# A row normalization with a loop of tiles: statistics combined by bn_aggr on VectorE instead of on GpSimd, in groups of four rows, and the last store issued as two DMAs

## The chip, the cores and the metric

The kernel runs on one core of a Trainium2 chip. The metric is the device time of the program in microseconds; the time before is the median of three runs. DVE is VectorE, ACT is ScalarE, POOL is GpSimd, SP is SyncE. TensorE does nothing here. 16 DMA engines move data between the memory that holds `x` and `out` and the on-chip memory of 128 partitions.

## The reference

```python
batch, seq, dim = 32, 512, 1024          # x: float32, eps = 1e-5
mean = np.mean(x, axis=-1, keepdims=True)
var = np.var(x, axis=-1, keepdims=True)
return ((x - mean) / np.sqrt(var + eps)).astype(np.float32)
```

There are 32 x 512 = 16384 rows of 1024 numbers, each normalized by itself: 67.11 MB are read and 67.11 MB are written.

## The kernel before

The rows are cut into 18 tiles (`TILES`): fifteen of 8 rows per partition, then one of 4 and two of 2. A tile of K rows has K x 128 rows of `x`, and each partition holds K rows that lie side by side in memory, so a load or a store is one DMA with one run of K x 4 KB per partition. Loads go into a ring of 32 rows per partition (`XRING`, four tiles of 8), results into a ring of their own of 16 rows (`YRING`, two tiles of 8). A load is issued by SP (line 124), a store by ACT's queue (line 129). The order of the instructions on each engine is the order of the program; nothing is rescheduled.

The loop in line 123 goes over the tiles. For each it issues the load, calls `group` for up to `GROUP` = 8 rows at a time (so once per tile), and issues the store. `group` does this:

- Line 77: DVE runs `bn_stats` twice per row, on 512 numbers each. Each call leaves six numbers: for the even and for the odd half of its input a count, a mean and a sum of squared deviations. A row so has four means and four sums.
- Lines 88 to 103: POOL combines them with nine instructions for all rows of the group. `pool_sum` adds four terms in two steps; the negated mean, the deviations of the four means from it, their squares times 256 and the sums of squares follow.
- Line 105: ACT takes the square root of the variance plus eps. Line 109: DVE takes the reciprocal. Line 111: POOL multiplies negated mean and reciprocal.
- Line 113: ACT writes each row as row x `rstd` + `nmr`, one instruction of 1024 numbers per partition and row.

A load waits until ACT and DVE have read the rows that it overwrites, four tiles back. The first `yr` of a tile waits until the store two tiles back has landed. On DVE the reciprocal of a tile stands ahead of the statistics of the next one, so DVE is at most one group ahead of ACT.

Of the kernel before, what the change touches and what calls it, by code (L numbers as in the profile page):

```python
# [1 line left out]

# [4 lines left out]


TILES = (8, 8, 8, 8, 8, 8, 8, 8, 8, 8, 8, 8, 8, 8, 8, 4, 2, 2)  # L10

XRING = 32
YRING = 16

GROUP = 8


def place(tiles, ring):

    plan, row, pos = [], 0, 0  # L20
    for K in tiles:
        if pos + K > ring:
            pos = 0
        plan.append((K, row, pos))
        row += K
        pos += K
    return plan


@with_exitstack  # L30
def kernel(
    ctx: ExitStack,
    tc: tile.TileContext,
    x: bass.AP,
    eps: bass.AP,
    out: bass.AP,
):
    nc = tc.nc
    P = nc.NUM_PARTITIONS
    eps_val = float(eps) if not isinstance(eps, bass.AP) else 1e-5  # L40

    x2 = x.flatten_outer_dims()
    o2 = out.flatten_outer_dims()
    N, D = x2.shape
    BN_MAX = nc.vector.BN_STATS_FMAX
    NSUB = D // BN_MAX
    assert sum(TILES) * P == N

    rings = ctx.enter_context(tc.tile_pool(name="rings", bufs=1))
    st = ctx.enter_context(tc.tile_pool(name="st", bufs=4))  # L50

    fdt = mybir.dt.float32
    AF = mybir.ActivationFunctionType
    ALU = mybir.AluOpType

    xr = rings.tile([P, XRING, D], fdt)
    yr = rings.tile([P, YRING, D], fdt)
    eps_t = rings.tile([P, 1], fdt)

    def rows_of(a, row, K):  # L60
        return a[row * P : (row + K) * P].rearrange("(p k) d -> p k d", p=P)

    def pool_sum(o, terms):
        G = terms.shape[1]
        half = st.tile([P, GROUP, 2], fdt, name="half")
        nc.gpsimd.tensor_tensor(  # L66
            out=half[:, :G], in0=terms[:, :, 0:2], in1=terms[:, :, 2:4], op=ALU.add
        )
        nc.gpsimd.tensor_tensor(  # L69
            out=o, in0=half[:, :G, 0], in1=half[:, :G, 1], op=ALU.add  # L70
        )

    def group(xs, ys, G):
        stats = st.tile([P, GROUP, NSUB, 6], fdt, name="stats")
        for k in range(G):
            for s in range(NSUB):
                nc.vector.bn_stats(  # L77
                    out=stats[:, k, s, :],
                    in_=xs[:, k, s * BN_MAX : (s + 1) * BN_MAX],
                )  # L80

        H = 2 * NSUB
        parts = stats[:, :G].rearrange("p g s (h c) -> p g (s h) c", h=2)
        mean4, m2 = parts[:, :, :, 1], parts[:, :, :, 2]
        nmean = st.tile([P, GROUP], fdt, name="nmean")
        dev = st.tile([P, GROUP, H], fdt, name="dev")
        ss = st.tile([P, GROUP], fdt, name="ss")
        pool_sum(nmean[:, :G], mean4)
        nc.gpsimd.tensor_scalar(  # L89
            out=nmean[:, :G], in0=nmean[:, :G], scalar1=-1.0 / H, scalar2=None, op0=ALU.mult  # L90
        )
        nc.gpsimd.tensor_tensor(  # L92
            out=dev[:, :G],
            in0=mean4,
            in1=nmean[:, :G].unsqueeze(2).to_broadcast([P, G, H]),
            op=ALU.add,
        )
        nc.gpsimd.tensor_mul(out=dev[:, :G], in0=dev[:, :G], in1=dev[:, :G])  # L98
        nc.gpsimd.tensor_scalar(  # L99
            out=dev[:, :G], in0=dev[:, :G], scalar1=float(D // H), scalar2=None, op0=ALU.mult  # L100
        )
        nc.gpsimd.tensor_tensor(out=dev[:, :G], in0=dev[:, :G], in1=m2, op=ALU.add)  # L102
        pool_sum(ss[:, :G], dev[:, :G])
        std = st.tile([P, GROUP], fdt, name="std")
        nc.scalar.activation(  # L105
            out=std[:, :G], in_=ss[:, :G], func=AF.Sqrt, bias=eps_t, scale=1.0 / D
        )
        rstd = st.tile([P, GROUP], fdt, name="rstd")
        nc.vector.reciprocal(out=rstd[:, :G], in_=std[:, :G])  # L109
        nmr = st.tile([P, GROUP], fdt, name="nmr")  # L110
        nc.gpsimd.tensor_mul(out=nmr[:, :G], in0=nmean[:, :G], in1=rstd[:, :G])  # L111
        for k in range(G):
            nc.scalar.activation(  # L113
                out=ys[:, k, :],
                in_=xs[:, k, :],
                func=AF.Identity,
                bias=nmr[:, k : k + 1],
                scale=rstd[:, k : k + 1],
            )

    with tc.manual_schedule():
        nc.vector.memset(eps_t, eps_val)  # L122
        for (K, row, xp), (_, _, yp) in zip(place(TILES, XRING), place(TILES, YRING)):
            nc.sync.dma_start(out=xr[:, xp : xp + K, :], in_=rows_of(x2, row, K))
            for g in range(0, K, GROUP):
                G = min(GROUP, K - g)
                a, b = xp + g, yp + g
                group(xr[:, a : a + G, :], yr[:, b : b + G, :], G)
            nc.scalar.dma_start(out=rows_of(o2, row, K), in_=yr[:, yp : yp + K, :])  # L129


# [1 line left out]
_INS = ['x', 'eps']  # L133
_OUTS = [((32, 512, 1024), 'float32')]

_NUMBERS = {'eps': 1e-05}


# [26 lines left out]
```

## Time and profile before

| what | value |
|---|---|
| median of 3 runs | 318.06 us (318.04 to 318.25) |
| profiled execution, its own time | 318.04 us |
| its span, first to last instruction | 316.3 us |
| DVE busy | 155.6 us, 256 bn_stats of 677 ns |
| ACT busy | 153.4 us, 128 rows of 1227 ns |
| POOL busy | 41.5 us, 184 instructions |
| DMA | 134.26 MB, mean 425 GB/s |
| last store issued, last instruction's end | 309.77 us, 316.3 us |

Busy time is that of one engine in the span; the DMA rate is that of all 16 DMA engines together. Times in the views count from the start of the span. An engine's busy share says little on a kernel whose engines wait for one another, so the views that matter here are those which show what is never idle, and what ends last.

### The profile page before, as it was taken

To read this page: it belongs to the slowest core of one execution; us is meant where nothing else is said; L and a number is where in the kernel's file an instruction comes from. 1 tells how busy PE (TensorE), PEld (TensorE's weight loads), DVE (VectorE), ACT (ScalarE), POOL (GpSimd) and SP (SyncE) were. 2 spreads that over 40 slices of the span, in tenths; PEclk is the share of its full clock that TensorE was granted. 3 is DMA by queue.
4 is the path that set the end of the run, shared out by engine and by line. 5 is a ranking of instruction groups with operands and counts; after the bars stand their busy time and mean duration, and the time that the engine had idled before them with its cause. 6 is when DMAs were issued, how large, how long until landed. Compare 5 with 4: busy or idle time off the path is not lost.

```text
span 316.3 us, 749 instructions
## 1 busy us (share of the span) xinstructions
DVE 155.6 (49%) x275; ACT 153.4 (49%) x147; POOL 41.5 (13%) x184
## 2 busy tenths in 40 slices
DVE  0387595708347092560916519074290834841330
ACT  1006591190642908338092470915619065769651
POOL 0002202100201102020020200202002020112220
DMA  8999989999999999999999999999999999999996
GB/s 332 423 439 431 431 386 435 435 435 427 439 424 443 419 452 411 448 414 452 419 448 423 448 427 432 427 435 435 427 443 419 448 408 433 456 406 441 450 407 274
DMA packets 5189, 134.26 MB, mean 425 GB/s; under 512 B 576, under 2 KB 576, under 8 KB 576
## 3 DMA queue, kind: packets, MB, share of 16 engines
q1 hardware_dynamic: 2592, 67.11, 49.7%
q10 hardware_dynamic: 2592, 67.11, 49.2%
q14 instruction: 5, 0.04, 0.0%
HBM read 67.11 MB, written 67.11 MB: 424 GB/s over the span
## 4 chain that ended last, share of the span: by engine, by line
DMA 65%; ACT 23%; DVE 7%; POOL 2%; issue 1%; ACTq 0%; POOLq 0%
DMA out_dram<-yr 61%; ACT yr L113 23%; DVE stats L77 7%; DMA xr<-in_x_dram 4%; POOL half L66 0%; ACT std L105 0%; POOL dev L99 0%; POOL dev L102 0%; POOL dev L92 0%; POOL nmean L89 0%; POOL dev L98 0%; POOL nmean L69 0%; POOL ss L69 0%; DVE rstd L109 0%; ACTq L129 0%
## 5 line engine op out<-in xcount | busy, mean ns | idle before, releaser
L113 ACT ACTIVATE yr<-xr,nmr,rstd 128x1024 f32<-128x1024 f32 x128 | 146.7, 1227 | 117.8 <-DMA out_dram<-yr 115.7
L77 DVE BATCH_NORM_STATS2 stats<-xr 128x6 f32<-128x512 f32 x256 | 153.4, 677 | 12.2 <-DMA xr<-in_x_dram 12.2
L109 DVE RECIPROCAL rstd<-std 128x8 f32<-128x8 f32 (+2 forms) x18 | 3.5, 197 | 138.4 <-ACT std L105 138.4
L66 POOL TENSOR_TENSOR half<-stats 128x16 f32<-128x16 f32 (+2 forms) x18 | 4.2, 232 | 161.3 <-DVE stats L77 161.3
L105 ACT ACTIVATE std<-ss,eps_t 128x8 f32<-128x8 f32 (+2 forms) x18 | 5.4, 300 | 37.6 <-POOL ss L69 31.5
L111 POOL TENSOR_TENSOR nmr<-nmean,rstd 128x8 f32<-128x8 f32 (+2 forms) x18 | 3.6, 202 | 92.5 <-DVE rstd L109 92.5
L99 POOL TENSOR_SCALAR dev<-dev 128x32 f32<-128x32 f32 (+2 forms) x18 | 5.2, 291 | 1.6
L102 POOL TENSOR_TENSOR dev<-dev,stats 128x32 f32<-128x32 f32 (+2 forms) x18 | 4.5, 251 | 1.5
L92 POOL TENSOR_TENSOR dev<-stats,nmean 128x32 f32<-128x32 f32 (+2 forms) x18 | 4.3, 238 | 1.5
L98 POOL TENSOR_TENSOR dev<-dev 128x32 f32<-128x32 f32 (+2 forms) x18 | 4.2, 234 | 1.4
L89 POOL TENSOR_SCALAR nmean<-nmean 128x8 f32<-128x8 f32 (+2 forms) x18 | 4.2, 231 | 1.6
L66 POOL TENSOR_TENSOR half<-dev 128x16 f32<-128x16 f32 (+2 forms) x18 | 3.9, 214 | 1.4
L69 POOL TENSOR_TENSOR ss<-half 128x8 f32<-128x8 f32 (+2 forms) x18 | 3.6, 202 | 1.4
L69 POOL TENSOR_TENSOR nmean<-half 128x8 f32<-128x8 f32 (+2 forms) x18 | 3.6, 201 | 1.4
L105 ACT ACT_TABLE_LOAD x1 | 1.3, 1283 | 0.9 <-DVE eps_t L122 0.9
L122 DVE MEMSET eps_t<- 128x1 f32 x1 | 0.1, 59 | 0.8 <-PEq L146 0.8
L146 POOL MEMSET const-float32-0.0<- 128x1 f32 x1 | 0.1, 100 | 0.2 <-issue 0.2
L146 POOL MEMSET const-bfloat16-1.0<- 128x1 bf16 x1 | 0.1, 102 | 0.0
L146 POOL MEMSET const-uint8-127<- 128x1 uint8 x1 | 0.1, 102 | 0.0
L146 POOL MEMSET const-float32-1.0<- 128x1 f32 x1 | 0.1, 99 | 0.0
## 6 DMA issues: line engine op xcount, KB each, us to landing
xr<-in_x_dram SPq DMA_DIRECT2D x15, 4096.0 KB, 32.4
out_dram<-yr ACTq DMA_DIRECT2D x15, 4096.0 KB, 29.4
xr<-in_x_dram SPq DMA_DIRECT2D x1, 2048.0 KB, 32.9
xr<-in_x_dram SPq DMA_DIRECT2D x2, 1024.0 KB, 45.3
out_dram<-yr ACTq DMA_DIRECT2D x1, 2048.0 KB, 9.6
out_dram<-yr ACTq DMA_DIRECT2D x2, 1024.0 KB, 7.0
```

What stands on the lines that cost most here:

```text
L66: nc.gpsimd.tensor_tensor(out=half[:, :G], in0=terms[:, :, 0:2], in1=terms[:, :, 2:4], op=ALU.add)
L69: nc.gpsimd.tensor_tensor(out=o, in0=half[:, :G, 0], in1=half[:, :G, 1], op=ALU.add)
L77: nc.vector.bn_stats(out=stats[:, k, s, :], in_=xs[:, k, s * BN_MAX : (s + 1) * BN_MAX],)
L89: nc.gpsimd.tensor_scalar(out=nmean[:, :G], in0=nmean[:, :G], scalar1=-1.0 / H, scalar2=None, op0=ALU.mult)
L92: nc.gpsimd.tensor_tensor(out=dev[:, :G], in0=mean4, in1=nmean[:, :G].unsqueeze(2).to_broadcast([P, G, H]), op=ALU.add,)
L98: nc.gpsimd.tensor_mul(out=dev[:, :G], in0=dev[:, :G], in1=dev[:, :G])
L99: nc.gpsimd.tensor_scalar(out=dev[:, :G], in0=dev[:, :G], scalar1=float(D // H), scalar2=None, op0=ALU.mult)
L102: nc.gpsimd.tensor_tensor(out=dev[:, :G], in0=dev[:, :G], in1=m2, op=ALU.add)
L105: nc.scalar.activation(out=std[:, :G], in_=ss[:, :G], func=AF.Sqrt, bias=eps_t, scale=1.0 / D)
L109: nc.vector.reciprocal(out=rstd[:, :G], in_=std[:, :G])
L111: nc.gpsimd.tensor_mul(out=nmr[:, :G], in0=nmean[:, :G], in1=rstd[:, :G])
L113: nc.scalar.activation(out=ys[:, k, :], in_=xs[:, k, :], func=AF.Identity, bias=nmr[:, k : k + 1], scale=rstd[:, k : k + 1],)
```

## The change

Four things change. The ten POOL instructions per group go. In place of the first nine, DVE runs `bn_aggr` once per row, directly behind the row's two `bn_stats`; it leaves the row's mean and variance. In place of the tenth, DVE forms `nmr` with one `scalar_tensor_tensor`. `GROUP` becomes 4, so a tile of 8 rows is done in two groups, each with its own `std`, `rstd` and `nmr`. The store of the last tile (2 rows) is issued as two DMAs, one of partitions 0 to 119 and one of partitions 120 to 127; all other stores stay as they are. The order of SP's loads is the same.

```diff
-GROUP = 8
+GROUP = 4
...
     def group(xs, ys, G):
         stats = st.tile([P, GROUP, NSUB, 6], fdt, name="stats")
+        mv = st.tile([P, GROUP, 2], fdt, name="mv")
         for k in range(G):
             for s in range(NSUB):
                 nc.vector.bn_stats(
...
                 )
+            nc.vector.bn_aggr(out=mv[:, k, :], in_=stats[:, k, :, :])
-        pool_sum(nmean[:, :G], mean4)
...
-        pool_sum(ss[:, :G], dev[:, :G])
         std = st.tile([P, GROUP], fdt, name="std")
         nc.scalar.activation(
-            out=std[:, :G], in_=ss[:, :G], func=AF.Sqrt, bias=eps_t, scale=1.0 / D
+            out=std[:, :G], in_=mv[:, :G, 1], func=AF.Sqrt, bias=eps_t, scale=1.0
         )
...
-        nc.gpsimd.tensor_mul(out=nmr[:, :G], in0=nmean[:, :G], in1=rstd[:, :G])
+        nc.vector.scalar_tensor_tensor(
+            out=nmr[:, :G],
+            in0=mv[:, :G, 0],
+            scalar=-1.0,
+            in1=rstd[:, :G],
+            op0=ALU.mult,
+            op1=ALU.mult,
+        )
...
-            nc.scalar.dma_start(out=rows_of(o2, row, K), in_=yr[:, yp : yp + K, :])
+            dst, src = rows_of(o2, row, K), yr[:, yp : yp + K, :]
+
+            cuts = ((0, 120), (120, P)) if (row + K) * P == N else ((0, P),)
+            for a, b in cuts:
+                nc.scalar.dma_start(out=dst[a:b], in_=src[a:b])
```

More of the change, by code (lines that the diff above doesn't have):

```diff
@@ L61, in rows_of @@
         return a[row * P : (row + K) * P].rearrange("(p k) d -> p k d", p=P)
[L63 to L71, printed above, removed]
     def group(xs, ys, G):
         stats = st.tile([P, GROUP, NSUB, 6], fdt, name="stats")
+        mv = st.tile([P, GROUP, 2], fdt, name="mv")
         for k in range(G):
@@ L80, in group @@
                 )
[L82 to L87, printed above, removed]
-        pool_sum(nmean[:, :G], mean4)
[L89 to L102, printed above, removed]
-        pool_sum(ss[:, :G], dev[:, :G])
+            nc.vector.bn_aggr(out=mv[:, k, :], in_=stats[:, k, :, :])
         std = st.tile([P, GROUP], fdt, name="std")
         nc.scalar.activation(
-            out=std[:, :G], in_=ss[:, :G], func=AF.Sqrt, bias=eps_t, scale=1.0 / D
+            out=std[:, :G], in_=mv[:, :G, 1], func=AF.Sqrt, bias=eps_t, scale=1.0
         )
```

## The prediction

> **What bounds the kernel now.** I read the profile page first, its slices and queues, to see which resource is never idle.
>
> ```profile
> DVE 155.6 (49%) x275; ACT 153.4 (49%) x147; POOL 41.5 (13%) x184
> ...
> DMA  8999989999999999999999999999999999999996
> ...
> q1 hardware_dynamic: 2592, 67.11, 49.7%
> q10 hardware_dynamic: 2592, 67.11, 49.2%
> ...
> DMA 65%; ACT 23%; DVE 7%; POOL 2%; issue 1%; ACTq 0%; POOLq 0%
> ```
>
> No compute engine is busy for half of the span, while the 16 DMA engines are at 9 tenths from the second slice to the last but one, and the two queues (q1 loads, q10 stores) fill 98.9% of them. Next came the busy time by stretches, cut so that each loss of DMA time shows (columns: stretch and length, then DVE, ACT, POOL, clock, DMA share, GB/s).
>
> ```profile
> 0.00:1.70 1.70, 0.06 (x1) 0.77 (x1) 0.19 (x4) 1.00 0.00 0
> ...
> 37.00:41.00 4.00, 2.19 (x5) 1.97 (x3) 1.32 (x6) 1.00 1.03 352
> ...
> 60.00:220.00 160.00, 78.96 (x139) 78.62 (x75) 20.74 (x89) 1.00 1.01 434
> ...
> 304.00:308.00 4.00, 0.17 (x1) 1.12 (x3) 2.07 (x10) 1.00 1.00 430
> 308.00:312.00 4.00, 0.00 (x0) 1.74 (x2) 0.00 (x0) 1.00 0.97 410
> ...
> 313.00:313.50 0.50, 0.00 (x0) 0.00 (x0) 0.00 (x0) 1.00 0.47 197
> 313.50:314.00 0.50, 0.00 (x0) 0.00 (x0) 0.00 (x0) 1.00 0.39 164
> 314.00:314.50 0.50, 0.00 (x0) 0.00 (x0) 0.00 (x0) 1.00 0.12 49
> 314.50:315.00 0.50, 0.00 (x0) 0.00 (x0) 0.00 (x0) 1.00 0.04 16
> 315.00:316.30 1.30, 0.00 (x0) 0.00 (x0) 0.00 (x0) 1.00 0.00 0
> ```
>
> At the steady 434 GB/s the 134.22 MB take 309.3 us. Before the first byte lie 1.70 us, after the last 1.30. The stretch at 37 to 41, where stores first join loads, loses 4 x (434 - 352) / 434 = 0.76. From 313.0 to 315.0 the engines run dry one after another, and 2.0 us do the work of about 0.5: 1.5 lost. The small dips in between add up to 1.7. Sum: 309.3 + 1.7 + 1.3 + 0.76 + 1.5 + 1.7 = 316.3, the span. So compute has no term of its own, and the end is set by those DMA engines that run dry last. In the trace's landing records of the last store, the first engine reports at 313.54, fourteen have by 314.68, and the last two at 315.14 and 315.18. I call those two the late engines.
>
> Last I read the chain's end (start, length, what), to see how far the last tile's arithmetic is from mattering.
>
> ```profile
> 295.97 4.64 ACT yr L113 x4
> ...
> 301.45 2.48 DVE stats L77 x4
> 303.94 0.07 issue
> 304.00 0.22 POOL half L66
> ...
> 307.37 2.37 ACT yr L113 x2
> ```
>
> This chain runs through the last tile's statistics and POOL, but only because it follows instructions: the share of 1.00 at 304 to 308 and 0.97 at 308 to 312 shows that earlier stores were still occupying the engines meanwhile.
>
> **The combination moves from POOL to DVE: 0 us while loads run.** Removed are ten POOL instructions per group, about 0.2 to 0.3 us each, nine of them in the way of std (from 304.00 to 306.53 in the last tile). Added are one bn_aggr per row, 128 in all, and one scalar_tensor_tensor per group in place of the POOL product. Neither is in this trace. From below they are bounded by the 59 ns memset, from above by bn_stats at 677 ns; I take 0.2 us, since the nearest rows are the tiny DVE reciprocals (166 ns for 128x2, 203 for 128x8), plus 0.07 for the wait on the statistics just before. A half tile's statistics then take 4 x (2 x 0.6 + 0.27) = 5.9 us on DVE, and what follows (std 0.30, reciprocal 0.18, product 0.2, hand-overs 0.2) 0.9: 13.6 per tile. A tile's DMA time with its load is 2 x 4.19 MB at 434 GB/s, 19.3 us, which covers it; at the upper bound, 17.4, still.
>
> **GROUP 8 to 4: 0 us, thin in the tail.** ACT now does std, four rows, std, four rows. The second std and the DVE work behind it stand between the halves, 0.9 us per tile, ahead of the second half of yr, so of the tile's store on ACT's queue and of SP's load that waits for those rows. Against it stand ACT's 115.7 us of waits for stores to land, 14 times, 8.3 each. Where loads have ended that cover goes: a store alone takes 4.19 MB / 434 = 9.7 us, less than the 13.6. There only a lead helps. With the landings of this trace, from that of the 12th store: 270.75 + 0.1 + half a yr 4.6 + 0.9 + 5.9 + 0.9 + 5.9 + 0.9 + half a yr 4.6 = 294.5 for the issue of the 15th store, the last of 8 rows (now 292.54). Issue to first byte was about 1.0 at the start (issue at 0.72, nothing moved until 1.70), so bytes flow from 295.5. The 14th store lands at 295.86 on its last engine, whose data ended some 0.3 earlier: the margin is 0. But the first store now leaves earlier, at 13.1 + 5.9 + 0.9 + 5.9 + 0.9 + 4.6 = 31.3 instead of 35.63. I estimate that a quarter of these 4.3 us is left as margin here, 1 us, since both the chain's start and the store ahead move. Early engines, which end 1.6 us before the late ones, may then idle some 0.6 unseen. So 0; at the upper bound of bn_aggr, 0.75 with its wait, the two halves grow by 8 x 0.48 = 3.8 us, +2.8, and near +5 if the 14th store is late as well.
>
> **The last tile's chain gets shorter: 0 us.** Statistics with aggregation 4 x 0.6 + 2 x 0.27 = 2.9 and 0.9 behind them, against 5.9 now (301.45 to 307.37): the last store is issued 2.1 us earlier, near 307.7. But the store ahead of it lands at 312.73 on its last engine, and the last store's bytes cannot start before. What could be won is the dip at 308 to 312, 4 x 24 / 434 = 0.22 us; I count none, since the dip lies on early engines.
>
> **The last store in two: +0.31 us.** Each DMA of the trace has 144 packets (2592 over 18), 128 of data and 16 tiny, so each engine carries 8 partitions. A partition of the last store is 8 KB, at 430 GB/s over 16 engines 0.305 us. 120 partitions in portions of 8 use 15 engines and leave one empty; the other 8 partitions are a ninth packet for each of 8 engines. If a late engine is among the eight, the end moves by +0.31. If neither is, it stays; if one of the two is the empty one, the other, 0.04 us ahead of it, sets the end: -0.04. With two late engines out of 16 and eight ninth packets, the chance of at least one hit is about 3 in 4. The worst split is 120 over 8 engines, 15 packets each and then one more: 8 x 0.305 = +2.44. I take +0.31 and keep -0.04 and +2.44. The second issue costs ACT another 0.34 us, behind which nothing is queued, and which passes while the first part moves.
>
> [...] The trace does not name its engines, so no row here confirms which are late.
>
> **Code fetches: 0 us, from -0.9 to +0.9.** The page shows a third queue, q14 instruction, with 5 packets of 8 KB in the span. In the trace each takes 0.31 us of one engine and the packet behind it is 0.12 to 0.61 longer, so one engine falls behind by 0.43 to 0.92. With POOL's stream gone and DVE's longer, these fetches hit other engines at other times. A late engine may lose its delay or get another.
>
> **Sum.** The profiled execution took 318.04 us with a span of 316.3 (1.74 around it), 0.02 under the median of 318.06. 318.04 + 0.31 = 318.35 us. About 0.2%, 0.64 us, is what a measurement of this kernel can tell from no change.
>
> **Rivals.** (a) Slower by the split: the 120 partitions go over 8 engines, 318.04 + 2.44 = 320.5. It decides as soon as any engine gets more than two extra packets. For it: 8 is the largest portion that divides both 120 and the engines; against it: 15 portions of 8 keep what every row shows. (b) Slower by a fetch: a late engine with a ninth packet also gets a new fetch, 0.31 + 0.43 to 0.92, so 318.8 to 319.3. For it: five fetches meet 16 engines. (c) Faster: the two late engines owe their delay to fetches that move, and the empty engine was one of them; the end falls by 0.7 to 1.3, towards the mean landing of about 314.0: 316.8 to 317.4. Against it: both must be relieved. (d) Slower by starved engines: bn_aggr with its wait takes over 0.4 us (0.27 + 1 / 8), and the 15th store comes too late; +2.8 to +5, so 321 to 323. For it: the margin is thin, and DVE is slower per tile than a store alone; against it: no small DVE row exceeds 203 ns.
>
> **Chances.** Forecast, within 0.64 us: 0.65. (a) 0.05, (b) 0.13, (c) 0.10, (d) 0.07. So faster 0.10, same 0.65, slower 0.25. The range reaches over (b) and to the near edge of (c), 317.5 to 319.3, and leaves out (a), (d) and most of (c).
>
> **What would show it.** Right: GB/s near 434 from 60 to 220, DVE some 190 us busy (155.6 + 128 x 0.2 + 48 small ones), POOL almost none, the last store issued before 309, the landings of the last store ending 0.3 later, the smaller DMA with 8 data packets. Wrong: DMA shares below 0.9 between 280 and 310 (starved), landings spread over more than 3 us (the split went badly), or a last landing before 314.7.

## Result and the profile after

The changed kernel takes 321.80 us (median of 4 runs, 321.31 to 323.10) against 318.09 beside it: ratio 1.0122, 95% interval 1.0092 to 1.0152, slower by 3.7 us. That is above the forecast of 318.35 us, and above its range, which ended at 319.3. Ratios here leave out runs over 1.5% above the fastest of their kernel, which matters for the kernels that scatter; medians take all runs. The profiled execution took 321.86 us with a span of 320.1.

From the page of the changed kernel: busy times, DMA slices, queues, and the two new groups of instructions.

```profile
DVE 186.9 (58%) x451; ACT 158.1 (49%) x162; POOL 0.2 (0%) x4
...
DMA  8999999999999999999999999999999999999994
...
q1 hardware_dynamic: 2592, 67.11, 49.2%
q10 hardware_dynamic: 2599, 67.11, 49.1%
q14 instruction: 6, 0.05, 0.0%
...
L72 DVE BATCH_NORM_AGGREGATE mv<-stats 128x2 f32<-128x12 f32 x128 | 26.7, 209 | 4.4
...
L81 DVE SCALAR_TENSOR_TENSOR nmr<-mv,rstd 128x4 f32<-128x4 f32 (+1 forms) x33 | 5.4, 162 | 1.1
```

The compute is as forecast (bn_aggr 209 ns against 0.2 us, DVE 187 us against some 190). The DMA engines still look full, so the loss must be in how they are full. The 2599 packets of q10 also tell how the last store was shared out: 17 x 144 + (120 + 15) + (8 + 8) = 2599, so its parts ran on 15 and on 8 engines.

The stretches of the changed kernel (columns as before: stretch, length, DVE, ACT, POOL, clock, DMA share, GB/s):

```profile
60.00:220.00 160.00, 96.61 (x233) 81.49 (x84) 0.00 (x0) 1.00 1.00 432
220.00:280.00 60.00, 36.46 (x88) 30.44 (x32) 0.00 (x0) 1.00 1.00 430
...
308.00:312.00 4.00, 0.00 (x0) 1.11 (x1) 0.00 (x0) 1.00 0.97 403
312.00:316.00 4.00, 0.00 (x0) 0.00 (x0) 0.00 (x0) 1.00 0.89 264
316.00:318.00 2.00, 0.00 (x0) 0.00 (x0) 0.00 (x0) 1.00 0.24 94
318.00:320.10 2.10, 0.00 (x0) 0.00 (x0) 0.00 (x0) 1.00 0.03 12
```

Two things stand out. In the middle the share is 1.00 while GB/s are lower than 434: engines are busy with packets that take longer. From 312 to 316 it is the same, drastically: 0.89 busy for 264 GB/s. And the last engines straggle until 318.7. The trace's packet records give the sum. Most packets of 32 KB take 1213 ns, most of 8 KB 309 ns; what a packet takes beyond that I call slow time.

| us, mean over 16 engines | before | after | more |
|---|---|---|---|
| slow time of packets, 41 to 290 us | 0.14 | 0.80 | 0.66 |
| engines without work, 285 to 310 us | 0.00 | 0.59 | 0.59 |
| slow time of packets, from 290 us on | 0.02 | 1.36 | 1.34 |
| mean end of the last packets | 313.72 | 316.25 | 2.53 |
| the last engine behind that mean | 1.12 | 2.45 | 1.33 |

2.53 + 1.33 = 3.86 us, against 3.82 between the two profiled times. Four mechanisms were in question: **F**, code fetches on the engine that ends last; **G**, the half tiles that make the 15th store late; **S**, slow packets of the split store; **P**, the moment at which the first store is issued.

### The profile page after: what moved, and what is told of

It reads as the page before. It is cut to its first block, busy times and chain, and to the rows that moved or that the text cites. A ratio compares the mean times of both kernels' runs of the same rounds, so it can differ in the third digit from the quotient of the medians.

```text
span 320.1 us, 730 instructions
## 1 busy us (share of the span) xinstructions
DVE 186.9 (58%) x451; ACT 158.1 (49%) x162; POOL 0.2 (0%) x4
## 3 DMA queue, kind: packets, MB, share of 16 engines
q10 hardware_dynamic: 2599, 67.11, 49.1%
## 4 chain that ended last, share of the span: by engine, by line
DMA 64%; ACT 22%; DVE 9%; issue 1%; another core or an unknown queue 0%; ACTq 0%
DMA out_dram<-yr 60%; ACT yr L90 21%; DVE stats L68 7%; DMA xr<-in_x_dram 4%; DVE mv L72 1%; ACT std L75 1%; DVE rstd L79 1%; DVE nmr L81 1%; ACTq L110 0%; ACTq L90 0%
## 5 line engine op out<-in xcount | busy, mean ns | idle before, releaser
L90 ACT ACTIVATE yr<-xr,nmr,rstd 128x1024 f32<-128x1024 f32 x128 | 148.4, 1229 | 115.2 <-DMA out_dram<-yr 106.9
L68 DVE BATCH_NORM_STATS2 stats<-xr 128x6 f32<-128x512 f32 x256 | 159.2, 664 | 12.8 <-DMA xr<-in_x_dram 12.8
L79 DVE RECIPROCAL rstd<-std 128x4 f32<-128x4 f32 (+1 forms) x33 | 5.9, 178 | 100.7 <-ACT std L75 100.7
L72 DVE BATCH_NORM_AGGREGATE mv<-stats 128x2 f32<-128x12 f32 x128 | 26.7, 209 | 4.4
L75 ACT ACTIVATE std<-mv,eps_t 128x4 f32<-128x4 f32 (+1 forms) x33 | 9.6, 292 | 35.1 <-DVE mv L72 34.6
L81 DVE SCALAR_TENSOR_TENSOR nmr<-mv,rstd 128x4 f32<-128x4 f32 (+1 forms) x33 | 5.4, 162 | 1.1
```

The source lines that it names most:

```text
L68: nc.vector.bn_stats(out=stats[:, k, s, :], in_=xs[:, k, s * BN_MAX : (s + 1) * BN_MAX],)
L72: nc.vector.bn_aggr(out=mv[:, k, :], in_=stats[:, k, :, :])
L75: nc.scalar.activation(out=std[:, :G], in_=mv[:, :G, 1], func=AF.Sqrt, bias=eps_t, scale=1.0)
L81: nc.vector.scalar_tensor_tensor(out=nmr[:, :G], in0=mv[:, :G, 0], scalar=-1.0, in1=rstd[:, :G], op0=ALU.mult, op1=ALU.mult,)
L90: nc.scalar.activation(out=ys[:, k, :], in_=xs[:, k, :], func=AF.Identity, bias=nmr[:, k : k + 1], scale=rstd[:, k : k + 1],)
```

## Experiments

Each edit is to the kernel named; "one store" means the last store as a single DMA.

**1. The change with one store.**

```diff
-            cuts = ((0, 120), (120, P)) if (row + K) * P == N else ((0, P),)
+            cuts = ((0, P),)
```

> The changed kernel with its last store issued as one DMA again; everything else as changed. Four theories are kept apart. S (split): the packets of the 120-partition store take 0.3 to 1.2 us each instead of 0.31 in the trace of after, so the split costs far more than a ninth packet: 319.5 to 320.3 us here, last packets back at 0.31. F (code fetch): DVE's longer code is fetched over one DMA engine, which ends last: only the ninth packet is saved, 321.3 to 321.6. G (groups): the 15th store is issued too late by the DVE chain, engines idle 0.6 us on average at 293 to 295: also 321.3 to 321.6. P (phase): the first store arrives at the engines just as they change from the third load to the fourth, some engines then alternate loads and stores against the rest and are slowed: 321.3 to 321.6 too.

322.07 us (320.26 to 325.85; ratio 1.0087, 1.0055 to 1.0120), above what any of the four had forecast. Without the split the time did not fall, so S is not the main cause. Unexpected was the scatter of over 5 us, and in the profiled run (323.19) 3.06 us of slow time per engine between 41 and 290.

**2. The kernel before with the split alone.** The edit is the `cuts` of the change, put into the kernel before.

> The kernel before with only the last store split into 120 and 8 partitions. S: packets of 0.4 us and more in the last 4 us, +0.5 to +1.5, so 318.6 to 319.6 us. F, G and P: at most the ninth packet, +0.0 to +0.3, so 318.1 to 318.4.

318.81 us beside 318.42 (ratio 1.0011, 1.0000 to 1.0022): inside S's range, and so small that the interval touches no change. The slow packets themselves are plain. Stretches of the profiled run:

```profile
312.00:314.00 2.00, 0.00 (x0) 0.00 (x0) 0.00 (x0) 1.00 0.92 262
314.00:316.00 2.00, 0.00 (x0) 0.00 (x0) 0.00 (x0) 1.00 0.44 156
```

Engines are 0.92 busy for 262 GB/s: 1.00 us of slow time per engine at the end. The profiled run is the slowest of the twelve (319.61 us; its last packets end at 316.4 instead of 314.8), so 0.4 us, the difference of the medians, is the better price for S.

**3. bn_aggr, but groups of 8 and one store.**

```diff
-GROUP = 4
+GROUP = 8
```

> bn_aggr and the product on DVE as in the change, but groups of 8 rows and one last store. F: DVE still has some 420 instructions, 3 to 4 code fetches on one engine, so 319.0 to 320.5 us. G: the chain's second half is gone, no idle engines at 293 to 295, 318.0 to 318.5. P: the first store leaves near 34 us, inside the fourth load as before, so few slow packets, 318.0 to 318.5. S: 318.0 to 318.5.

319.21 us (ratio 1.0023, 1.0012 to 1.0035), inside F's 319.0 to 320.5: slow time 0.19, no engine without work, but the last engine 2.11 behind the mean end. Three fetches of DVE's code lie in its span, one more than before, for +0.8 us.

**4. POOL's combination in groups of 4, one store.** The edit is `GROUP = 4` in the kernel before.

> The statistics combined on POOL as before, but in groups of 4 rows, one last store. F: DVE's code is about as long as before, 2 fetches, so 318.0 to 318.5 us. G: the chain of half tiles is even longer than with bn_aggr (POOL's nine instructions twice per tile), engines idle before the 15th store, 318.5 to 320. P: the first store leaves near 32 us, close to the change of loads: slow packets and out-of-step engines are likely, 319 to 321. S: 318.0 to 318.5.

320.00 us (319.79 to 320.07; ratio 1.0045, 1.0029 to 1.0061): G's upper end. Its first store left at 33.9 and there were no slow packets (0.19), so this is G nearly by itself: queue 14 had 8 packets instead of 5, but the last engine ended only 0.53 us behind the mean. Stretches of this run:

```profile
293.00:294.00 1.00, 1.00 (x3) 1.00 (x1) 0.00 (x0) 1.00 0.35 147
294.00:295.00 1.00, 1.00 (x2) 1.00 (x2) 0.00 (x0) 1.00 0.08 33
295.00:296.00 1.00, 0.08 (x1) 0.26 (x1) 0.64 (x3) 1.00 0.04 16
```

The engines had nothing to do for 1.9 us each, because the 15th store was issued only at 295.29.

**5. The change with one store, the first tile in one group of 8.**

```diff
-            for g in range(0, K, GROUP):
-                G = min(GROUP, K - g)
+            step = 8 if row == 0 else GROUP
+            for g in range(0, K, step):
+                G = min(step, K - g)
```

> As the changed kernel with one last store, but the first tile alone is one group of 8 rows, so the first store leaves near 34 us instead of 30.4; tiles from the second on in groups of 4. P (the moment of the first store decides): the slow packets between 41 and 290 us, 3.1 us per engine in the run with groups of 4 and one store, fall below 0.3, runs agree within 1 us, and F's code fetches alone are left: 319.5 to 320.5 us. If instead the groups of 4 in the steady state make the slow packets: 321 to 325 and a wide scatter as in that run.

320.36 us (319.94 to 320.73; ratio 1.0060, 1.0048 to 1.0072), slow time 0.25. One tile's grouping removed the slow packets and the scatter. Code fetches alone are not left, though: between 285 and 310 us the engines were without work for 0.8 us each.

**6. The reverse: experiment 3 with `step = 4 if row == 0 else GROUP`.**

> As the kernel with bn_aggr in groups of 8 and one store (319.2 us), but the first tile alone in groups of 4, so its store leaves near 30.4 us. P: slow packets of 0.5 us per engine and more between 41 and 290, 320 to 325 us with a wide scatter. If the groups of 4 of the steady state make them: 318.9 to 319.6, as without the edit.

322.91 us (319.78 to 324.44; ratio 1.0136, 1.0101 to 1.0170), slow time 3.80. Half tiles in the steady state are not needed for it.

**7. The kernel before with a longer DVE program.**

```diff
                 group(xr[:, a : a + G, :], yr[:, b : b + G, :], G)
+                if row < 13 * 8:
+                    for _ in range(12):
+                        nc.vector.memset(pad, 0.0)
```

> The kernel before plus 156 tiny memsets on DVE (12 behind the reciprocal of each of the first 13 tiles), which bring DVE's code to the length that it has after the change and move nothing else of the data path. F: DVE's code blocks in the span go from 2 to 4, all on the DMA engine that ends last, about 0.8 us each: +1.3 to +1.8, 319.4 to 320.0 us. Any theory without code fetches: 318.0 to 318.4.

319.89 us (319.75 to 320.35; ratio 1.0051, 1.0038 to 1.0063), +1.6, inside F's range. The added instructions, and queue 14, first of the kernel before and then of this run:

```profile
L132 DVE MEMSET pad<- 128x1 f32 x156 | 9.2, 59 | 9.5
```

```profile
q14 instruction: 5, 0.04, 0.0%
```

```profile
q14 instruction: 7, 0.06, 0.0%
```

156 instructions of 59 ns, on an engine that idles half the time, cost 1.6 us, while queue 14 carried two more packets of 8 KB, code of DVE by my reading. In the profiled run the engine that carries DVE's fetches ends at 316.95, some 2.6 us behind the mean (1.12 before). It also passes its delay on: the landing that the 15th tile waits for came 0.9 us later than before, and the engines were without work for 0.26 us each. So part of F's price goes by way of the tail.

**8. The kernel before with the last store in two halves of 64 partitions.**

> The kernel before with its last store split into 64 and 64 partitions instead of 120 and 8. S, as a matter of 15 engines that share out 120 partitions otherwise than 16 share out 128: with 64 and 64 all 16 engines carry 4 packets twice, no packet over 0.35 us, 318.0 to 318.4. If any second DMA at the end slows the packets: as with 120 and 8, 318.6 to 319.2.

319.18 us (318.46 to 320.83; ratio 1.0027, 1.0014 to 1.0039): my expectation of no cost missed. In the profiled run, the slowest of the twelve, 92 of the last 128 packets of 8 KB take over 320 ns, 30 of them 627 to 631 ns, twice 309. So it is not the number of engines: queue 10 has 2608 packets, 17 x 144 + 2 x (64 + 16), 16 engines for each half. Nor is it a second store at the end as such: in the kernel before the last two stores ran side by side from 310.7 to 312.4 us, and no packet of 8 KB took over 319 ns. What is left is that each of these stores covers only some of the partitions (64, or 120 and 8); why that makes packets longer, no run here shows.

**9. Experiment 6 with only the first store issued later.**

```diff
+            if row == 0:
+                for _ in range(17):
+                    nc.scalar.activation(out=pad, in_=eps_t, func=AF.Identity, bias=eps_t, scale=1.0)
             dst, src = rows_of(o2, row, K), yr[:, yp : yp + K, :]
```

> The kernel with bn_aggr in groups of 8, the first tile in groups of 4, one last store (322.9 us, 319.8 to 324.4), plus 17 tiny ACT instructions between the first tile's rows and its store, so that this store alone is issued some 4 to 5 us later, at 34 to 36; the fifth load keeps its early time of 30.4. P, if the arrival of the first store decides: slow packets gone, 319.0 to 320.0 and little scatter. If the early fifth load or the half tiles decide: 321 to 325 as without the edit.

318.74 us (318.59 to 319.13; ratio 1.0014, 1.0006 to 1.0023): store at 35.66 instead of 30.49, slow time 0.17 instead of 3.80, 4.2 us less by adding work. It is the first store, not the fifth load.

**10. The whole change, first tile in one group of 8.** Experiment 5 with the split.

> The whole change, but with the first tile in one group of 8: the run with the first tile in one group (320.4 us) plus the split of the last store. S: slow packets in the last 4 us again and a ninth packet on a late engine, +0.3 to +0.8: 320.7 to 321.2 us. Were the split free: 320.4.

320.80 us (320.25 to 320.94; ratio 1.0070, 1.0056 to 1.0083): +0.44 over experiment 5, S again.

**11. The kernel before with shorter programs (half of each row left out of the statistics from the second tile on).** The edit passes `NSUB if row == 0 else 1` into `group` and lets `pool_sum` add two terms in one step.

> The kernel before with the second half of each row left out of the statistics from the second tile on (one bn_stats per row, 8 POOL instructions per group instead of 10); all loads, rows and stores stay. It shortens the code of DVE and POOL below their next block. F: one code block each for DVE, POOL and ACT in the span instead of 2, 2 and 1, so the last engine is 0.5 less behind: 317.3 to 317.7 us, faster than before. Any theory in which the compute chains set the time also gives less; one in which only the bytes do: 318.0 to 318.4.

317.56 us (317.36 to 318.52; ratio 0.9974, 0.9962 to 0.9987), F's forecast. Its queue:

```profile
q14 instruction: 3, 0.02, 0.0%
```

Three fetches instead of five, and the landings of the last store spread over 0.93 us instead of 1.64. The compute is shorter too, but the DMA engines were not waiting for it: between 285 and 310 us they had work without a break in both kernels.

**12. The kernel before with an early first store** (`1 if row == 0 else NSUB`, half of each row left out of the first tile's statistics alone).

> The kernel before with the second half of each row left out of the statistics of the first tile alone, so that its first store and fifth load leave near 30.5 us instead of 35.6; nothing else differs, POOL combines, groups are of 8 rows, the last store is one. P: slow packets of more than 0.5 us per engine between 41 and 290, a wide scatter, 319.5 to 325 us. If groups of 4 or bn_aggr were needed for the slow packets: 318.0 to 318.5.

324.49 us (324.10 to 325.28; ratio 1.0196, 1.0181 to 1.0212), slow time 5.28, with no bn_aggr, no group of 4 and no split, as P forecast except for the wide scatter. Stretches of this run, of which the kernel before has 433 to 434 in each:

```profile
60.00:100.00 40.00, 18.89 (x34) 18.28 (x19) 4.65 (x20) 1.00 1.01 429
100.00:140.00 40.00, 20.12 (x36) 19.52 (x20) 4.65 (x20) 1.00 1.01 428
140.00:180.00 40.00, 20.29 (x36) 19.46 (x20) 4.65 (x20) 1.00 1.00 422
180.00:220.00 40.00, 19.77 (x35) 18.50 (x19) 4.79 (x21) 1.00 1.00 421
220.00:260.00 40.00, 18.90 (x33) 17.81 (x18) 4.50 (x20) 1.00 1.00 423
```

**13 to 15. Experiment 12 with 4, 8 and 12 tiny ACT instructions ahead of the first store.** The edit is that of experiment 9 with other counts.

> The kernel before with its first store and fifth load made early (as in the run with the first store at 30.0: 324.5 us), plus 4 tiny ACT instructions ahead of the first store, so that it is issued near 31.2 us while the fifth load stays early. The third load's data ends at 31.9 and the fourth's begins at 31.4. If it matters whether the store's first bytes come before or after that change of loads (31.2 + 1 = 32.2, after it): 318 to 319. If the slow packets fall off step by step with the delay: 322 to 323.5.

> The same with 8 tiny ACT instructions, first store near 32.4 us. Change of loads: 318 to 319. Step by step: 320 to 322.

> The same with 12 tiny ACT instructions, first store near 33.7 us, about where the runs with a first store at 34 showed no slow packets: 318.0 to 319.0 by either.

| experiment | first store issued | median, us | slow time 41 to 290 |
|---|---|---|---|
| 12 | 29.97 | 324.49 | 5.28 |
| 13 | 30.88 | 319.27 | 0.17 |
| 14 | 32.15 | 318.78 | 0.17 |
| 15 | 33.42 | 318.44 | 0.16 |

Within 0.9 us of delay almost all of the slow time is gone, not step by step. What is left is small: experiment 13 still scatters (318.79 to 320.48, its profiled run being one of the two fastest), and its median of 319.27 lies just above the 318 to 319 that I expected. So in the profiled runs a first store issued at 29.97 to 30.50 was followed by 0.80 to 5.28 us of slow time per engine, one at 30.88 or later by 0.25 at most, but for 0.49 in experiment 8.

My reading, that the store's first bytes must not come before or into the change from the third load to the fourth, is not borne out. That change lies between 31.3 and 32.1 us in all these runs, and the first packets of the first store are recorded only 3.9 to 5.1 us after its issue, behind the change in the runs with slow packets (34.4 to 34.7) as in the others (35.8 and later).

## Why the prediction was wrong

**What held.** The middle is bound by DMA (share 1.00 from 60 to 280 us), bn_aggr costs 0.2 us (209 ns) and is hidden, and the ninth packet costs what was said: the late engine's first part of the last store landed at 318.78, its ninth packet at 319.08. How a store of 120 or of 8 partitions is shared out, no row of the kernel before shows, so the ninth packet was an estimate; the changed kernel's 2599 packets agree with it, 15 engines and 8.

**The largest step that failed, code fetches: the term was 0 with +0.9 as its bound; it is +1.6.** I let fetches fall on any of 16 engines. In these traces they do not. The packet records name no engine, but in both traces the engines can be told apart: on a busy engine each packet starts 3 or 4 ns before the one ahead of it ends, and of the 144 packets of a DMA each engine carries eight of data and one tiny one. Followed back from the end by these two marks, the packets of the kernel before lead from the engine that ends last, at 314.84, to two fetches (44.4 and 193.9 us). The records don't say whose code a fetch brings; I read these two as DVE's, since after the change four of the six fetches come in even steps of DVE's instructions. So this late engine was late because of code: 2 x 0.31 + 0.36 + 0.61 = 1.6 us. The other three fetches lie on engines that end at about 314.2 (89.2 and 302.8) and 313.8 (125.5). The second late engine, 314.81, carried none; its longest packet was one of a load, 3.21 us at 39.1, where stores first join loads. After the change DVE's fetches come at 38.3, 124.4, 210.6 and 296.6, every 125 to 130 instructions of DVE, again all on one engine: 0.44 + 3 x 0.31 and 0.40 + 0.53 + 0.53 + 0.54 in the packets behind them, 3.4 us. In experiments 5, 7 and 9 too the engine that ends last is the one with DVE's fetches. Experiments 3 and 7 show the price, 0.8 us for one more block and 1.6 for two, and 11 the reverse. DVE itself shows no wait for its code: after the change all its listed waits are for ACT's std (100.7 us), for loads (12.8) and, once at the start, 0.8. The delay shows on the DMA engine that fetches the code.

**A step with the wrong sign: the earlier first store was booked as a gain.** The part on GROUP put the first store at 31.3 instead of 35.63 and counted a quarter of the difference as margin. It left at 30.50, as these lines of the kernel before and of the changed kernel show:

```profile
35.63 0.38 ACTq L129 DMA_DIRECT2D out_dram<-yr  x1
```

```profile
30.50 0.40 ACTq L110 DMA_DIRECT2D out_dram<-yr  x1
```

The lead was worth little: in experiments 5 and 10, whose first stores left at 34.1 and 34.4, the engines were without work for 0.8 and 1.1 us at 285 to 310, against 0.6 after the change. And the moment was a bad one: P, some 1.0 us here (321.80 against the 320.80 of experiment 10) and up to 6 in experiment 12. Of P the forecast had no case.

**The split: one term of two.** The ninth packet was there, the doubled packets were not: +0.4 together (experiments 2 and 10), between my +0.31 and +2.44. Two halves cost more, +0.9 us (experiment 8: 319.18 against 318.29). Of slow packets the forecast had no term.

**The tail: the size was right, the end was not.** I wrote that early engines may idle some 0.6 unseen. They idled 0.59. First the 15th store of the kernel before, then the changed kernel's ACT around the second std of the 15th tile (start, length, engine, line, operation, and the wait ahead of it):

```profile
292.54 0.34 ACTq L129 DMA_DIRECT2D out_dram<-yr  x1
```

```profile
288.56 0.28 ACT L75 ACTIVATE std<-mv,eps_t 128x4 f32<-128x4 f32 x1
...
289.28 4.64 ACT L90 ACTIVATE yr<-xr,nmr,rstd 128x1024 f32<-128x1024 f32 x4 [0.44 <-DVE nmr L81]
293.95 0.34 ACTq L110 DMA_DIRECT2D out_dram<-yr  x1
```

The store left 1.41 us later, half of it from this gap and half from a later landing. What remains of experiment 5 after F is 320.36 - 319.89 = 0.5 us; I give it to G, without a run that isolates it beside bn_aggr. The last store did not leave near 307.7 either but at 309.14, since the last tile's statistics waited for their load until 303.06.

**The sum.** F 1.6 (experiment 7), G 0.5 (5 less 7), S 0.4 (10 less 5), P 1.0 (the change less 10): 3.5 us, of 3.7 measured. These are steps of one ladder from the kernel before to the change, so they must add up; the sum proves nothing. What supports the sizes is that S came out alike twice (experiments 2 and 10) and F's price per block twice (3 and 7). G and P are less certain: G is a remainder, and P stands on medians of runs that scatter by 1.8 us. Rival (d) named 321 to 323 by another mechanism, bn_aggr above 0.4 us, which did not happen; (b) had the right mechanism, but as an accident of one fetch, where all four of DVE's fetches lie on one engine.

**What stays open.** Why a first store issued at 29.97 to 30.50 us, and not one at 30.88, is followed by slow loads up to 290 us. In experiments 1 and 6, 191 and 181 of the loads' packets of 32 KB are over by more than 0.05 us between 41 and 290 us, and nearly three quarters of the loads' slow time falls in the first 6 us after a new store's first packet; stores carry little (0.2 us per engine). What slows them was not tried. No run beat the kernel before with the full computation; experiment 9 comes closest among those with bn_aggr (318.74 against 318.32).

## To carry to other kernels

When the DMA engines are saturated, look at which of the 16 ends last and why. Here each further fetch of DVE's code, one every 125 to 130 instructions in the changed kernel, cost about 0.8 us (experiments 3 and 7), even where the instructions themselves were free (156 memsets of 59 ns), and the DMA engine that carried the fetches ended last. Don't count an earlier start of a stream as a gain; try it, and look at GB/s where the DMA share is 1.00. Don't split a last store by partitions, since with two halves (experiment 8) 92 of the last 128 packets of 8 KB took over 320 ns instead of 309, 30 of them twice as long, and the kernel took 0.9 us more. A split by rows was not tried here.

## What the hardware showed unexpectedly

- Packets of 8 KB take 309 to 319 ns when a store covers all 128 partitions (the kernel before); when the last store covers 64 at a time, 92 of its last 128 take over 320 ns, 30 of them 627 to 631.
- An offset of 0.9 us in one store, 30 us into the run, changed the time by 5 us (324.49 against 319.27).
- The fetches that I read as DVE's come every 125 to 130 of its instructions in the changed kernel, all four on one DMA engine, and each puts it back by 0.84 to 0.85 us; in the kernel before there are two, of 0.67 and 0.92 us, also on one engine.
